# Moving the start addresses of the split weights and of the activations inside SBUF

## The chip, the cores and the metric

The kernel runs on one core of one Trainium2 chip. The metric is the device time of one execution in microseconds (us); lower is better. A change below 0.2% of it can't be told from no change.

## The reference, cut to what matters

Two layers of a network and a third block with its MLP are computed in float32 for 256 tokens of width 2048. Nearly all the arithmetic is in products of an activation (256 tokens by up to 8192 features) with a weight matrix that is read once from memory:

```
proj = h @ w_in                                      # layer 0: 2048 x 10272
return x + jnp.concatenate([y_a, y_b, y_m], axis=-1) @ w_out
...
proj = h @ w_in                                      # layer 1: 2048 x 4416
q = (rms_norm(c_q, mla_q_norm_w) @ mla_w_uq)
kv = (rms_norm(c_kv, mla_kv_norm_w) @ mla_w_ukv)
return x + jnp.concatenate([y_c, y_m], axis=-1) @ w_out
...
# block 2: retention with w_in (2048 x 12288) and w_out (4096 x 2048),
# then an MLP with w_up (2048 x 8192), relu squared, w_down (8192 x 2048)
```

Between the products stand norms, short convolutions, a state-space scan in chunks, and three kinds of attention.

## The kernel before

**One stream of weights.** `PLAN` lists every block of weight columns in the order in which it is worked. A block is a *job*; a job is cut into *sub-jobs* of at most 1024 float32 columns per partition. For each sub-job the kernel issues a DMA into a buffer `raw`, splits the weights into two parts, and multiplies. `run_stream` writes this order out by hand: splits run two sub-jobs ahead of the matmuls, DMAs up to three more.

**The split.** A product of float32 numbers is made from three products of a faster format (`F32R`): a number x is hi + lo, where hi is x cast to the format by ScalarE (ACT) and lo = x - hi comes from VectorE (DVE). `emit_split` puts both parts of a sub-job into one buffer `w` of 2112 elements per partition, hi from element `WOFF` = 20 and lo from `WOFF` + 1024. There are `N_SPLIT` = 4 such buffers. The activations are kept the same way: a `Feat` holds, for two blocks of 128 features, hi (256 tokens) and lo (256 tokens) side by side in a buffer of pool `unit`.

**Two layouts.** `emit_mm` issues the matmuls of a sub-job. The first operand of `mm` is the *stationary* one (128 x 128, loaded into the array before the matmul), the second the *moving* one (128 partitions by its columns):

```
if kind == "A":
    trio = ((dst, wh, xb), (dst[:, 0:256], wl, xh))
elif kind == "A3":
    trio = ((dst, wh, xh), (dst, wh, xl), (dst, wl, xh))
else:
    sh, sl = xh[:, t * 128:t * 128 + 128], xl[:, t * 128:t * 128 + 128]
    trio = ((dst, sh, wh), (dst, sh, wl), (dst, sl, wh))
```

- **A**: the weights are stationary. A pair of matmuls: weights hi against the activation's hi and lo together (512 columns), then weights lo against the activation's hi (256 columns).
- **A3**: the same in three matmuls of 256 columns (jobs `uq`, and half of `ukv`).
- **B**: the activations are stationary, the weights move: three matmuls of 512 columns (352, 384 or 288 in a few jobs, 256 in half of `ukv`).

In the trace, names stand as output<-moving,stationary: `g<-h,w` has the weights stationary, `g<-w,h`, `g<-w,y`, `g<-w,yr` and `g<-w,hid` have them moving (`g<-w,mem` and `g<-mem,w` are the same for the memory input).

**Where things lie.** Pools are laid one after the other in each partition. Their sizes give the start of each buffer; *phase* is that start modulo 256 bytes. The buffers of `w` are 8448 bytes (33 x 256), so all four start at one phase, 128. Buffers of `unit` (4096 bytes) and `half` (2048 bytes) hold the activations, and also all operands of the attentions; they start at one phase too, and slices inside them lie 512 or 1024 bytes apart. The pool of constants stands between `w` and `unit`, so its total size sets their phase. Before the change: both weight parts at 128 + 4 x 20 = 208, all buffers of `unit` and `half` at 192, the identity and other square constants (`sq`, `trs_r`) at 128, the key table `ks` at 160.

Of the kernel before, what the change touches and what calls it, by code (L numbers as in the profile page):

```python
# [19 lines left out]
N_HALF = 15  # L20
N_SPLIT = 4
AHEAD = 2
WOFF = 20
MLP_PARTS = (6, 5, 5)


# [89 lines left out]
def block_kernel(ctx, tc, a, out):  # L116
# [14 lines left out]
    def nm(s):  # L131
        serial[0] += 1
        return f"{s}_{serial[0]}"
# [10 lines left out]
    def C(shape, name, dt=F32):  # L144
        return cst.tile(shape, dt, name=name)

    def bank(shape, name):

        while free_banks[0] == 0:
            yield  # L150
        free_banks[0] -= 1
        return psb.tile(shape, F32, tag="b", name=nm(name))

    def rel():
        free_banks[0] += 1
# [20 lines left out]
    def mm(o, l, r, start, stop=True):  # L176
        nc.tensor.matmul(o, l, r, start=start, stop=stop, skip_group_check=True)  # L177
# [5 lines left out]
    def split_to(hi, lo, x):  # L183
        nc.scalar.copy(hi, x)  # L184
        tt(lo, x, hi.bitcast(F32), ALU.subtract)
# [2 lines left out]
    sq = C([128, 3, 128], "sq")  # L188
    ident, tri, cmask = (sq[:, i, :] for i in range(3))
    trs_r = C([128, 128], "trs_r", F32R)  # L190
    ones = C([128, 8], "ones")
    mhalf = C([128, 8], "mhalf")
    pv = C([128, NVEC], "pv")
    invf = C([128, 2], "invf")
    hv = C([128, 3, 32], "hv")
# [7 lines left out]
    o = 0  # L203
# [125 lines left out]
    def emit_split(m):  # L329
        s = subs[m]  # L330
        n, nc_ = s.n, s.job.ncols
        src = raws[(s.job.key, s.gi)][:, s.s0:s.s0 + n, :]

        hl = wsp.tile([128, 2112], F32R, tag="w", name=nm("w"))
        pitch = {352: 512, 288: 320}.get(nc_, nc_)
        hv_, lv_ = (hl[:, WOFF + i * 1024:WOFF + i * 1024 + n * pitch].rearrange(
            "p (k c) -> p k c", c=pitch)[:, :, 0:nc_] for i in range(2))
        split_to(hv_, lv_, src)
        splits[m] = (hv_, lv_)

# [34 lines left out]
    def run_stream():  # L375
# [15 lines left out]
        for m, s in enumerate(subs):  # L391
            if s.first and s.job.key in hooks:
                hooks[s.job.key]()
            while at["split"] < n and at["split"] <= m + (min(AHEAD, m) if m < n - 4 else 3):
                dma_to(at["split"])
                emit_split(at["split"])
                at["split"] += 1
            dma_to(min(at["split"] + 3, m + 3))
            drive(lambda: all(k in s.job.x.done for k in range(s.k0 + s.s0, s.k0 + s.s0 + s.n)))
            if m < n - 2:  # L400
                emit_mm(m)
                del splits[m]
                if s.last:
                    spawn(s.job.post(s.job.ps))
                step_tasks()
# [45 lines left out]
    def rstd_from(dst, sums, n, ncols):  # L451
        v = S([128, ncols])
        ts(v, sums, 1.0 / n, EPS, ALU.mult, ALU.add)
        nc.gpsimd.tensor_tensor(dst, v, mhalf[:, 0:ncols], ALU.pow)  # L454
# [25 lines left out]
    def feat_rstd(dst, sqs, n):  # L480

        acc = sqs[0]
        nc.gpsimd.tensor_tensor(acc[:, 0:2, :], acc[:, 0:2, :], acc[:, 2:4, :], ALU.add)
        nc.gpsimd.tensor_tensor(acc[:, 0, :], acc[:, 0, :], acc[:, 1, :], ALU.add)
        yield
        yield
        ps = yield from bank([128, 2, 128], "fs")
        for t in range(2):
            mm(ps[:, t, 0:8], acc[:, 0, t * 128:(t + 1) * 128], ones, start=(t == 0))
        yield  # L490
        rstd_from(dst, ps[:, :, 0], n, 2)
        rel()
        yield
# [119 lines left out]
    def prep_mem():  # L613
        sqs = []
        for u in range(4):
            memt.alloc(u)
            for kp, nk in ((0, 1), (1, 1), (2, 2)) if u == 0 else ((0, 2), (2, 2)):
                memt.write_scaled(u * 4 + kp, nk, lambda k: memu[u][:, kp + k, :],
                                  lambda k: col("mem_norm_w", u * 4 + kp + k))
                memt.mark(u, kp, nk)  # L620
                yield
            s = U([128, 4, 256], F32, "msq")
            act(s, memu.pop(u), AF.Square)
            add_up(sqs, s)
        yield from feat_rstd(stat[:, RM, :], sqs, D)
        rbm = H([128, 256], F32, "rbm")
        yield from bcast_rows(rbm, stat[:, RM, :])
        L0["rbm"] = rbm

    def prep_x():  # L630
        yield from wait(7)
        xu, sqs = [], []
        for u in range(4):
            xu.append(load_t(a["xt"], u, "xt"))
            yield from wait(2)
            s = U([128, 4, 256], F32, "xsq")
            act(s, xu[u], AF.Square)
            add_up(sqs, s)
        r0 = S([128, 2])
        yield from feat_rstd(r0, sqs, D)  # L640
        rb0 = H([128, 256], F32, "rb0")
        yield from bcast_rows(rb0, r0)
        yield
        for u in range(4):
            h0.alloc(u)
            for kp in (0, 2):
                nc.gpsimd.tensor_tensor(xu[u][:, kp:kp + 2, :], xu[u][:, kp:kp + 2, :],
                                        rb0.unsqueeze(1).to_broadcast([128, 2, 256]), ALU.mult)
                yield
                h0.write_scaled(u * 4 + kp, 2, lambda k: xu[u][:, kp + k, :],  # L650
                                lambda k: col("norm0_w", u * 4 + kp + k))
                h0.mark(u, kp, 2)
# [185 lines left out]
    def ssd_group(g):  # L838
# [73 lines left out]
        yield  # L912
        rg = S([128, 2])
        yield from feat_rstd(rg, [s2], 512)
        rb = H([128, 256], F32, "rbg")
        yield from bcast_rows(rb, rg)
# [488 lines left out]
    for entry in PLAN:  # L1405
        key = entry[0]
        kind, rest = key[0], key[1:]
        n = len(entry[3])
# [114 lines left out]
```

## Time and profile before

| | |
|---|---|
| time of three runs | 2674.33, 2674.76, 2675.19 us (median 2674.76) |
| the profiled execution | 2674.39 us, of which 2672.6 us is the span of its instructions |
| granted TensorE clock | 0.999 of the full 2.4 GHz |
| TensorE matmul (PE) busy | 2651.7 us, 14136 matmuls |
| TensorE weight load (PEld) busy | 2280.1 us |
| DVE, ACT, POOL busy | 1638.7, 1299.1, 141.6 us |
| DMA | 488.86 MB, mean 183 GB/s |

A matmul's busy time in the trace overlaps that of the next one, since they are pipelined. How long one really takes of TensorE's time is read from the distance between the starts of neighbours: in a merged row of the timeline, the length less the duration of the last matmul, divided by the count less one.

### The profile page before, as it was taken

What the parts mean: (1) busy time and instruction counts of PE and PEld (TensorE: products, weight loads), DVE (VectorE), ACT (ScalarE), POOL (GpSimd) and SP (SyncE); (2) the same over time, 40 slices, a digit from 0 to 9 for tenths busy, and PEclk for the clock granted to TensorE, in tenths of its full rate; (3) what the DMA queues carried; (4) which work ended last, traced back from release to release, by engine and by line L of the source; (5) the groups of instructions that cost most, each with busy time, mean ns of one, the idle gap of its engine ahead of it and who ended that gap; (6) DMA issues with size and microseconds to landing.
All of it is one profiled execution on the core that took longest, in us unless ns stands there. A gap on an engine that the chain in (4) does not pass through costs nothing.

```text
span 2672.6 us, 34737 instructions
## 1 busy us (share of the span) xinstructions
PE 2651.7 (99%) x14136; PEld 2280.1 (85%) x14136; DVE 1638.7 (61%) x2066; ACT 1299.1 (49%) x1772; POOL 141.6 (5%) x104
## 2 busy tenths in 40 slices
PE   8999999999999999999999999999999999999998
PEld 7998888888899999888888888888888888888886
DVE  6757787655546887646565555555555545545554
ACT  5556555544444666544444343444455434534543
POOL 4100232000000000000000000000000000000000
PEclk9999999999999999999999999999999999999999
DMA  7454444565545444455444455454455555555553
GB/s 268 173 188 170 158 158 159 188 221 193 187 152 204 148 150 174 173 190 206 176 174 183 178 189 186 179 193 172 178 186 190 190 189 189 189 190 188 189 207 139
DMA packets 74688, 488.86 MB, mean 183 GB/s; under 512 B 8864, under 2 KB 10656, under 8 KB 20384
## 3 DMA queue, kind: packets, MB, share of 16 engines
q1 hardware_dynamic: 74528, 486.64, 50.2%
q8 instruction: 110, 1.80, 0.3%
q14 instruction: 50, 0.41, 0.0%
HBM read 484.51 MB, written 2.10 MB: 182 GB/s over the span
## 4 chain that ended last, share of the span: by engine, by line
PE 97%; ACT 1%; DVE 1%; DMA 0%; issue 0%; SPq 0%; POOLq 0%; POOL 0%; DVEq 0%; ACTq 0%
PE g L177 92%; PE tr L425 1%; PE ro L177 1%; PE at.s L177 1%; ACT w L184 0%; DMA raw<-in_mem_v_dram 0%; PE rs L177 0%; PE at.o L177 0%; DVE w L162 0%; PE yd L177 0%; PE seg L177 0%; DVE xbc L171 0%; PE ma.s L177 0%; PE ma.o L177 0%; PE at.t L1168 0%
## 5 line engine op out<-in xcount | busy, mean ns | idle before, releaser
L162 DVE TENSOR_TENSOR w<-raw,w 128x1024 fp32r<-128x1024 f32 (+4 forms) x929 | 1115.3, 1211 | 850.1 <-ACT w L184 849.4
L184 ACT CAST w<-raw 128x1024 fp32r<-128x1024 f32 (+4 forms) x929 | 936.6, 1026 | 681.2 <-PE g L177 663.4
L177 PE MATMUL g<-h,w 128*128 128x512 f32 (+1 forms) x6144 | 1084.3, 337 | 1.0 <-DVE qx L162 1.0
L177 PEld LDWEIGHTS g<-h,w 128*128 128x128 f32 x6144 | 941.8, 188 | 125.8 <-issue 2.0
L177 PE MATMUL g<-w,h 128*128 128x512 f32 (+3 forms) x2208 | 468.0, 372 | 0.0
L177 PEld LDWEIGHTS g<-w,h 128*128 128x128 f32 x2208 | 392.5, 188 | 65.9
L177 PE MATMUL g<-w,hid 128*128 128x512 f32 x1536 | 356.6, 394 | 0.8 <-DVE x L171 0.8
L177 PEld LDWEIGHTS g<-w,hid 128*128 128x128 f32 x1536 | 288.5, 188 | 68.1 <-DVE x L171 1.3
L177 PE MATMUL g<-w,y 128*128 128x512 f32 x1152 | 269.9, 395 | 0.0
L177 PEld LDWEIGHTS g<-w,y 128*128 128x128 f32 x1152 | 215.6, 188 | 49.6 <-ACT y L184 0.4
L284 ACT COPY low<-g 128x512 f32<-128x512 f32 x100 | 58.8, 588 | 343.5 <-PE g L177 343.5
L177 PE MATMUL g<-w,yr 128*128 128x512 f32 x768 | 179.8, 395 | 0.0
L177 PEld LDWEIGHTS g<-w,yr 128*128 128x128 f32 x768 | 144.0, 188 | 33.0
L162 DVE TENSOR_TENSOR x<-x,g 128x512 f32<-128x512 f32 x48 | 30.8, 684 | 71.3 <-PE g L177 71.3
L162 DVE TENSOR_TENSOR blk<-g,low 128x512 f32<-128x512 f32 x100 | 68.3, 683 | 0.4 <-PE g L177 0.4
L177 PE MATMUL g<-w,mem 128*128 128x512 f32 x192 | 50.2, 420 | 8.6 <-ACT mem L174 7.2
L1303 POOL TENSOR_TENSOR s<-s,mhalf 128x1 f32<-128x1 f32 x16 | 22.6, 1412 | 608.9 <-DVE s L166 608.9
L177 PEld LDWEIGHTS g<-w,mem 128*128 128x128 f32 x192 | 37.9, 201 | 19.6 <-ACT mem L174 8.1
L177 PE MATMUL g<-cq,w 128*128 128x256 f32 x432 | 54.5, 282 | 0.0
L454 POOL TENSOR_TENSOR stat<-s,mhalf 128x2 f32<-128x2 f32 x7 | 10.1, 1446 | 828.9 <-DVE s L168 828.9
L177 PEld LDWEIGHTS g<-cq,w 128*128 128x128 f32 x432 | 52.3, 188 | 0.1
L174 ACT ACT_TABLE_LOAD x28 | 35.9, 1283 | 20.5 <-PE pre L177 10.5
(264 smaller groups left out, 1450.3 us busy)
## 6 DMA issues: line engine op xcount, KB each, us to landing
raw<-in_w_in_dram SPq DMA_DIRECT2D x96, 1024.0 KB, 4.8
raw<-in_ret_w_in_dram SPq DMA_DIRECT2D x96, 1024.0 KB, 4.8
raw<-in_mlp_w_up_dram SPq DMA_DIRECT2D x64, 1024.0 KB, 4.8
raw<-in_mlp_w_down_dram SPq DMA_DIRECT2D x64, 1024.0 KB, 4.8
raw<-in_w_out_dram SPq DMA_DIRECT2D x48, 1024.0 KB, 4.8
raw<-in_ret_w_out_dram SPq DMA_DIRECT2D x32, 1024.0 KB, 4.8
raw<-in_w_in_dram SPq DMA_DIRECT2D x12, 704.0 KB, 4.0
raw<-in_mem_k_dram SPq DMA_DIRECT2D x8, 1024.0 KB, 4.8
```

The lines of the kernel that those rows point to most:

```text
L162: nc.vector.tensor_tensor(o, x, y, op)
L174: nc.scalar.activation(o, x, f, **kw)
L177: nc.tensor.matmul(o, l, r, start=start, stop=stop, skip_group_check=True)
L184: nc.scalar.copy(hi, x)
L284: nc.scalar.copy(low, ps[:, :, 256:512])
L425: nc.tensor.transpose(ps[:, i, t * 128:(t + 1) * 128], src(t, kp + i), ident)
L454: nc.gpsimd.tensor_tensor(dst, v, mhalf[:, 0:ncols], ALU.pow)
L1303: nc.gpsimd.tensor_tensor(r, vv, mhalf[:, 0:1], ALU.pow)
```

## The change

`WOFF` goes. The weight parts now start at offsets that depend on the layout: jobs of kinds in `A_KINDS` (weights stationary) put hi at element 1048 and lo at element 12, the others (weights moving) hi at 1032 and lo at 8. Two constants of 8 columns, `ones` and `mhalf`, become halves of one tile `om` of 8 columns, which makes the pool of constants 32 bytes smaller; the sums over partitions in `feat_rstd` use 4 columns instead of 8.

```diff
-WOFF = 20
+PHASES = {"A": (1024 + 24, 12), "B": (1024 + 8, 8)}
+A_KINDS = ("mk", "B", "C", "xs", "sz", "sc", "mq", "mz", "uq", "ukv", "zc", "q", "k", "up")
...
-    ones = C([128, 8], "ones")
-    mhalf = C([128, 8], "mhalf")
+    om = C([128, 8], "om")
+    ones, mhalf = om[:, 0:4], om[:, 4:8]
...
-        hv_, lv_ = (hl[:, WOFF + i * 1024:WOFF + i * 1024 + n * pitch].rearrange(
-            "p (k c) -> p k c", c=pitch)[:, :, 0:nc_] for i in range(2))
+        hv_, lv_ = (hl[:, o:o + n * pitch].rearrange("p (k c) -> p k c", c=pitch)[:, :, 0:nc_]
+                    for o in PHASES["A" if s.job.key[0] in A_KINDS else "B"])
...
-            mm(ps[:, t, 0:8], acc[:, 0, t * 128:(t + 1) * 128], ones, start=(t == 0))
+            mm(ps[:, t, 0:4], acc[:, 0, t * 128:(t + 1) * 128], ones, start=(t == 0))
```

On every engine the instructions stand in the same order before and after; only the width of those twelve small sums and of two memsets changes, and the addresses:

| operand, start modulo 256 bytes | before | after |
|---|---|---|
| weights, stationary: hi / lo | 208 / 208 | 224 / 176 |
| weights, moving: hi / lo | 208 / 208 | 160 / 160 |
| activations and all buffers of `unit` and `half` | 192 | 160 |
| `ks` | 160 | 128 |
| `sq`, `trs_r` | 128 | 128 |

## Rows read from the trace of the kernel before

**Rows 1.** The page: span; busy time of each engine, share, instructions.

```profile
span 2672.6 us, 34737 instructions
PE 2651.7 (99%) x14136; PEld 2280.1 (85%) x14136; DVE 1638.7 (61%) x2066; ACT 1299.1 (49%) x1772; POOL 141.6 (5%) x104
```

**Rows 2.** The page: the chain that ended last, by engine.

```profile
PE 97%; ACT 1%; DVE 1%; DMA 0%; issue 0%; SPq 0%; POOLq 0%; POOL 0%; DVEq 0%; ACTq 0%
```

**Rows 3.** Waits of PE: who for whom, total us, times, longest.

```profile
PE g L177 <- ACT mem L174: 7.2, 3, 5.9
PE ma.t L534 <- DVE p L166: 1.3, 1, 1.3
```

**Rows 4.** Groups of PE by shape: busy us, mean ns, then idle before.

```profile
L177 PE MATMUL g<-h,w 128*128 128x512 f32 x3072 | 1073.6, 393 | 1.0 <-DVE qx L162 1.0
L177 PE MATMUL g<-h,w 128*128 128x256 f32 x3072 | 863.0, 281 | 0.0
L177 PE MATMUL g<-w,h 128*128 128x512 f32 x1536 | 361.3, 395 | 0.0
L177 PE MATMUL g<-w,hid 128*128 128x512 f32 x1536 | 356.6, 394 | 0.8 <-DVE x L171 0.8
L177 PE MATMUL g<-w,y 128*128 128x512 f32 x1152 | 269.9, 395 | 0.0
L177 PE MATMUL g<-w,yr 128*128 128x512 f32 x768 | 179.8, 395 | 0.0
L177 PE MATMUL g<-cq,w 128*128 128x256 f32 x432 | 54.5, 282 | 0.0
L177 PE MATMUL g<-w,mem 128*128 128x512 f32 x192 | 50.2, 420 | 8.6 <-ACT mem L174 7.2 <-DVE mem L171 0.9 <-DVE w L162 0.4
L177 PE MATMUL g<-mem,w 128*128 128x512 f32 x128 | 44.7, 393 | 0.0
L177 PE MATMUL g<-ck,w 128*128 128x256 f32 x192 | 28.5, 284 | 0.0
```

**Rows 5.** Timeline of PE, layout A in the MLP: start, length, group, count.

```profile
1959.80 100.47 PE L177 MATMUL g<-h,w 128*128 128x256 f32 x579
```

**Rows 6.** Timeline of PE, layout B in the MLP.

```profile
2089.80 90.51 PE L177 MATMUL g<-w,hid 128*128 128x512 f32 x390
```

**Rows 7.** Busy time by stretch in A and B: PE, PEld, DVE, ACT, POOL; PEclk.

```profile
1954.00:2084.00 130.00, 130.00 (x753) 115.28 (x752) 74.97 (x80) 65.53 (x80) 1.60 (x1) 1.00 0.53 188
2090.00:2180.00 90.00, 90.00 (x390) 73.03 (x389) 45.05 (x40) 35.52 (x36) 0.00 (x0) 1.00 0.55 198
```

**Rows 8.** Timeline of PE: a job of layout A3 (`uq`).

```profile
886.56 4.42 PE L177 MATMUL g<-cq,w 128*128 128x256 f32 x36
```

**Rows 9.** Timeline of PE: six matmuls `ro`, both operands at phase 192.

```profile
1621.77 0.39 PE L177 MATMUL ro<-vh,sh 128*128 128x512 f32 x1
1622.00 0.40 PE L177 MATMUL ro<-vl,sh 128*128 128x512 f32 x1
1622.23 0.40 PE L177 MATMUL ro<-vh,sl 128*128 128x512 f32 x1
1622.47 0.39 PE L177 MATMUL ro<-vh,sh 128*128 128x512 f32 x1
1622.69 0.39 PE L177 MATMUL ro<-vl,sh 128*128 128x512 f32 x1
1622.93 0.40 PE L177 MATMUL ro<-vh,sl 128*128 128x512 f32 x1
```

**Rows 10.** Timeline of PE: moving constants at 128 against stationary data at 192.

```profile
717.63 1.03 PE L425 MATMUL tr<-sq,x 128*128 128x128 f32 x8
272.75 1.06 PE L177 MATMUL pre<-sq,dax 128*128 128x128 f32 x8
```

**Rows 11.** Timeline of PE: `ks` moving at 160 against 192, and the next.

```profile
1026.58 0.28 PE L177 MATMUL at.s<-ks,qs 128*128 128x256 f32 x1
1026.70 0.51 PE L177 MATMUL at.s<-kk,q 128*128 128x256 f32 x3
```

**Rows 12.** Timeline of PE: `rs`, plain float32, 256 columns, all at 192.

```profile
1277.70 1.02 PE L177 MATMUL rs<-q,k 128*128 128x256 f32 x4
```

**Rows 13.** Groups by shape: the split of a full sub-job on DVE and ACT.

```profile
L162 DVE TENSOR_TENSOR w<-raw,w 128x1024 fp32r<-128x1024 f32 x847 | 1043.9, 1242 | 777.4 <-ACT w L184 777.0
L184 ACT CAST w<-raw 128x1024 fp32r<-128x1024 f32 x847 | 874.0, 1049 | 642.0 <-PE g L177 628.3 <-DMA raw<-in_mem_v_dram 5.4 <-ACT w L184 5.0
```

## The prediction

> **What bounds the kernel now.** I read the page first: of the span, PE holds 99% [rows 1], and 97% of the chain that ended last is PE's [rows 2]. Then I asked what PE waits for: the longest entry is 7.2 us at the start, the next 1.3 us [rows 3]. So nothing that happens on DVE, ACT or the DMA queues sets the end; the time is the sum over 14136 matmuls of the distance from one start to the next. The change can only act by making that distance shorter or longer.
>
> These distances come from merged rows of the timeline. In layout A, 579 matmuls take 100.47 us [rows 5]; less the last one's 0.28 (its mean duration, [rows 4]) and over 578 steps that is 173.3 ns each, or 346.7 ns for a pair of 512 and 256 columns. In layout B, 390 matmuls take 90.51 us [rows 6]: (90.51 - 0.39) / 389 = 231.7 ns for 512 columns. A job of A3, all of 256 columns, has 36 in 4.42 us [rows 8]: (4.42 - 0.28) / 35 = 118.3 ns. With 118.3 for the 256 columns, the 512 of an A pair take 346.7 - 118.3 = 228.4 ns. The granted clock in both stretches is 1.00 [rows 7], the level of 2.4 GHz. At one column per cycle (an estimate) 512 columns would be 213.3 ns and 256 would be 106.7 ns. So there are some 15 ns over the stream in A's first matmul, 11.6 in its second, 18.4 in B. This excess is what an address could move.
>
> How much of it there is: A pairs are 3072 + 128 = 3200 and B matmuls of 512 columns 1536 + 1536 + 1152 + 768 + 192 = 5184 [rows 4]. Excess in A: 3200 x (346.7 - 320.0) = 85 us; in B: 5184 x 18.4 = 95 us. These 180 us, 6.7% of the time, are the ceiling of any gain in the two main layouts.
>
> **Does the excess depend on addresses?** While a matmul streams its moving operand, the stationary operand of the next one is loaded: PEld is busy 115.28 of 130 us in A [rows 7]. Two streams then read SBUF at once. One row says the excess is not a fixed price of a matmul: `rs` is plain float32, 256 columns, and takes (1.02 - 0.38) / 3 = 213 ns, which is just 512 cycles at 2.4 GHz (an estimate again), with no excess to be seen at the rounding of the row [rows 12]. Its columns enter at half the rate, and at half the rate the excess is gone. That speaks for two streams that get in each other's way at the full rate.
>
> The Trainium skill, page "TensorE: Matmul & The Clock Gate", section "Part 2: What happens when you issue a matmul", says otherwise: PE has two independent read ports, and loading the next weights takes nothing from the running matmul; its section "Back-to-back issue gap" gives N/2.4 + 2.5 ns, which would be 215.8 ns for 512 columns. The trace has 231.7 [rows 6], so the gap rule does not hold here; whether the port rule does is the question of the change. By that rule the sum would be zero.
>
> **The change part by part.** The unit of my argument is the difference d = phase of the moving operand less phase of the stationary operand that is loaded meanwhile, since this says where two streams that start together stand to each other.
>
> 1. *A, first matmul* (512 columns; the weights' lo is loaded). d was 192 - 208 = -16; it is 160 - 176 = -16. By d nothing changes: 0.
>
> 2. *A, second matmul* (256 columns; the next weights' hi is loaded). d was -16, it becomes 160 - 224 = -64. Two rows have d = -64: the transposes `tr` (identity at 128 moving, data at 192 stationary) with (1.03 - 0.27) / 7 = 108.6 ns, and `pre` with (1.06 - 0.28) / 7 = 111.4 ns [rows 10]. They have 128 columns, so it is the load that paces them and not the stream; but a 256-column matmul needs 106.7 ns for its stream and the same load of 128 columns beside it, so if neither is held up it takes what these rows take. From both sides, then: 108.6 (a gain of 9.7 ns) and 111.4 (a gain of 6.9), and at worst none. I take the middle of the two rows, 110.0, a gain of 8.3 ns. There are 3200 such matmuls in the A pairs, and in A3 two of three load hi next: 2/3 x (432 + 192) = 416 [rows 4]. 3616 x 8.3 = 30.0 us less.
>
> 3. *B* (5184 matmuls of 512). d was 208 - 192 = 16; it becomes 160 - 160 = 0. The row with d = 0 and 512 columns is `ro`: five steps from 1621.77 to 1622.93, 1.16 / 5 = 232.0 ns [rows 9], against 231.7 now. 5184 x 0.3 = 1.6 us more, which is nothing within the rounding. Bounds: the shortest step in those rows, 220 (from 1622.47 to 1622.69), and the longest, 240, though neither holds for many in a row.
>
> 4. *The narrower B jobs and the attentions.* The widths 352, 384 and 288 follow B: zero. In the attentions both operands lie in `unit` or `half` and move together; `ks` goes from 160 to 128 while its partner goes from 192 to 160. No d changes there: zero.
>
> 5. *The sums with 4 columns instead of 8, and the common tile `om`.* Twelve sums; the memsets stand at the very start, where PE waits for the memory input anyway [rows 3]. Zero.
>
> 6. *The split.* ACT and DVE write the same sizes to other addresses. DVE takes 1242 ns and ACT 1049 for a full sub-job [rows 13]; such a sub-job feeds PE for 8 pairs, 8 x 346.7 = 2774 ns. They could take half as long again before PE would wait; in the A stretch DVE is busy 74.97 of 130 us [rows 7]. Covered, zero; without this cover each nanosecond per split would cost 847 ns in all.
>
> Sum: 2674.39 (the profiled execution) - 30.0 + 1.6 = 2646.0. That execution lies 0.4 us under the median, so I forecast **2646 us**. With the two rows of step 2 as ends, its own range is 2674.4 - 35.1 + 1.6 = 2641 to 2674.4 - 25.0 + 1.6 = 2651; the rounding of the rows of `ro` (10 ns over five steps, 2 ns a matmul, 10 us in all) widens it to 2631 to 2661.
>
> **The rivals.**
>
> *B gains too.* If equal phases let the two streams run in step, so that they never ask for the same place at once, B's 231.7 falls as well. For it: `rs`, also at d = 0, shows no excess [rows 12]. Against it: `ro`, at the full rate, shows all of it [rows 9]. Price: down to the 213.3 of the bare stream it would be 95 us; halfway, 9.2 x 5184 = 48 us, the time 2646 - 1.6 - 48 = 2597. At the pace of A's first matmul (228.4) it would be 17 us, the time 2627.
>
> *Nothing happens.* The excess belongs to the full-rate stream alone, wherever it starts, and d plays no part. For it: 231.7 at d = 16, 232.0 at d = 0 and 228.4 at d = -16 are within 4 ns [rows 5, 6, 9]; `pre` and `tr` differ by 3 ns at one d [rows 10]. Time: 2675. The port rule of the Trainium skill, page "TensorE: Matmul & The Clock Gate", quoted above, says this too.
>
> *Slower: the moving stream dislikes the phase 160 itself.* Before the change one moving operand of TensorE lies at 160, `ks`: its step from 1026.58 to 1026.70 is 120 ns for 256 columns [rows 11], against 118.3 at 192 [rows 8]. If that is the phase and not the rounding, all moving streams now pay it: 1.7 ns per 256 columns, 5.1 per A pair (16 us) and 3.4 per B matmul (18 us), so 34 us more, 2709. It decides against the change as soon as a full-width B matmul takes 5.8 ns more than now with step 2 as I have it (30.0 us over 5184). Against it: the row's rounding alone is as large as the effect.
>
> **How the numbers follow.** My case: 0.40. B gains too: 0.22. Nothing: 0.18. Slower: 0.20, since the absolute phase of every moving stream changes and only one coarse row speaks to it. Faster by over 0.2% (5 us; less can't be told from no change in this kernel) is then 0.62, within 0.2% 0.18, slower 0.20. The range reaches to 2600, which leaves out the far part of the second case, and up to 2688, which takes in "nothing" and the nearer part of the slower case (half of its 34 us is 2692); about 0.1 is left out at either end.
>
> **What would show it.** In the profile after, PE should still wait for nothing. The A stretch of the MLP should have more matmuls per 100 us: 346.7 - 8.3 = 338.4 ns a pair, so about 591 in place of 579. The B stretch should keep its 390 in 90 us; 400 or more would show the second case, fewer than 386 the last. `uq` should fall from 118.3 to about 113 on the mean of its three. `ro`, `tr` and `pre`, whose d stays, should keep their steps; if they move, it is the absolute phase that counts and my unit d is wrong. The prediction is wrong if what a stream pays depends on where it starts rather than on its distance to the other, or if the rows with 128 columns say nothing about 256.

## The result and the profile after

| | before | after |
|---|---|---|
| median of four runs each | 2674.55 us (2673.77 to 2675.19) | 2643.15 us (2642.60 to 2643.27) |
| ratio, 95% interval | | 0.9882 [0.9865, 0.9899] |
| profiled execution, its span | 2674.39, 2672.6 us | 2643.22, 2641.4 us |
| its granted TensorE clock | 0.999 | 0.998 |

The kernel is 31.4 us faster, 1.2%. The forecast was 2646. The profile shows that the total came out near it for reasons other than those forecast.

The page of the kernel after: span, busy time of each engine, and the chain that ended last by engine. They answer to [rows 1, 2].

```profile
span 2641.4 us, 34737 instructions
...
PE 2620.3 (99%) x14136; PEld 2271.6 (86%) x14136; DVE 1639.1 (62%) x2066; ACT 1299.0 (49%) x1772; POOL 141.5 (5%) x104
...
PE 97%; ACT 1%; DVE 1%; DMA 0%; issue 0%; SPq 0%; POOLq 0%; POOL 0%; DVEq 0%; ACTq 0%
```

Waits of PE after (who for whom, total us, times, longest), for [rows 3]:

```profile
PE g L180 <- ACT mem L177: 7.3, 3, 5.8
PE ma.t L537 <- DVE p L169: 1.4, 1, 1.4
```

PE still has 99% of the span and 97% of the chain, and waits for nothing new; DVE, ACT and POOL are as busy as they were. So the 31 us come out of the distance from one matmul to the next. The timeline of PE after (start, length, group, count) shows where. The first row is uq [rows 8], the second layout B [rows 6], the third layout A in the place of [rows 5]; the other two are layout A elsewhere, where the pairs of the kernel before took 346.7 ns as well.

```profile
880.89 4.40 PE L180 MATMUL g<-cq,w 128*128 128x256 f32 x36
...
2072.71 107.60 PE L180 MATMUL g<-w,hid 128*128 128x512 f32 x474
...
1959.80 100.46 PE L180 MATMUL g<-h,w 128*128 128x512 f32 x590
...
494.82 85.44 PE L180 MATMUL g<-h,w 128*128 128x256 f32 x492
...
2414.83 105.55 PE L180 MATMUL g<-h,w 128*128 128x256 f32 x608
```

The reader takes the last matmul's duration off each length and divides by the count less one, as the prediction did. A merged row names the shape of its first matmul; in A the two shapes alternate, so with an odd count the last is of the same shape (0.39 or 0.28 us), with an even count of the other, and a pair comes out to some 0.2 ns. B: (107.60 - 0.39) / 473 = 226.7 ns, where it was 231.7. A in the first part of the MLP: twice (100.46 - 0.28) / 589, a pair of 340.2 ns, where it was 346.7. But A at 494 us and at 2414 us gives twice (85.44 - 0.39) / 491 and twice (105.55 - 0.39) / 607, pairs of 346.4 and 346.5, no faster than before to that accuracy. And `uq` takes (4.40 - 0.28) / 35 = 117.7 ns against 118.3.

Counted over all neighbours in the two traces by their starts (steps of B under 260 ns and pairs of A under 400, so that stalls are left out), the mean B step went from 231.65 to 226.91 ns and the mean A pair, from one 512-column start to the next, from 346.87 to 344.69. That is 4.74 x 5184 = 24.6 us from B and 2.18 x 3200 = 7.0 us from A, together 31.6 against the 31.4 measured. In A, 984 of 3059 pairs take at most 342 ns, where 4 did before, and 1902 still take 343 to 347. The small B widths hardly moved: 384 columns from 175.6 to 173.6 ns, 352 stayed at 160.0, 288 went from 130.5 to 131.7.

The busy time per group says the same more roughly. Groups of PE by shape after (busy us, mean ns, then idle before), for [rows 4]:

```profile
L180 PE MATMUL g<-h,w 128*128 128x512 f32 x3072 | 1066.7, 392 | 1.0 <-DVE qx L165 1.0
L180 PE MATMUL g<-h,w 128*128 128x256 f32 x3072 | 857.0, 279 | 0.0
...
L180 PE MATMUL g<-w,hid 128*128 128x512 f32 x1536 | 349.0, 389 | 0.8 <-DVE x L174 0.8
```

The B group falls by 356.6 - 349.0 = 7.6 us for 1536 matmuls, 4.9 each; the two A groups by 6.9 and 6.0 us for 3072 pairs, 4.2 a pair at the most. Busy times of pipelined matmuls overlap, so only the starts give the true size.

Last, the six `ro` of [rows 9], whose operands both lie at one phase before and after. Timeline of PE after:

```profile
1331.11 0.39 PE L180 MATMUL ro<-vh,sh 128*128 128x512 f32 x1
1331.34 0.39 PE L180 MATMUL ro<-vl,sh 128*128 128x512 f32 x1
1331.56 0.39 PE L180 MATMUL ro<-vh,sl 128*128 128x512 f32 x1
1331.79 0.39 PE L180 MATMUL ro<-vh,sh 128*128 128x512 f32 x1
1332.02 0.39 PE L180 MATMUL ro<-vl,sh 128*128 128x512 f32 x1
1332.24 0.39 PE L180 MATMUL ro<-vh,sl 128*128 128x512 f32 x1
```

Five steps in 1.13 us are 226 ns each, where they were 232. Nothing about these six changed but the absolute phase (192 to 160). By the prediction's own sign, absolute phase would then count. Or they follow the matmuls around them. The experiments had to settle that.

### The profile page after: what moved, and what is told of

Its sections match the earlier page's. It is cut to its first block, busy times and chain, and to the rows that moved or that the text cites. A ratio compares the mean times of both kernels' runs of the same rounds, so it can differ in the third digit from the quotient of the medians.

```text
span 2641.4 us, 34737 instructions
## 1 busy us (share of the span) xinstructions
PE 2620.3 (99%) x14136; PEld 2271.6 (86%) x14136; DVE 1639.1 (62%) x2066; ACT 1299.0 (49%) x1772; POOL 141.5 (5%) x104
## 4 chain that ended last, share of the span: by engine, by line
PE 97%; ACT 1%; DVE 1%; DMA 0%; issue 0%; SPq 0%; POOLq 0%; POOL 0%; DVEq 0%; ACTq 0%
PE g L180 92%; PE tr L428 1%; PE ro L180 1%; PE at.s L180 1%; DMA raw<-in_mem_v_dram 0%; ACT w L187 0%; PE rs L180 0%; PE at.o L180 0%; DVE w L165 0%; PE yd L180 0%; PE seg L180 0%; DVE xbc L174 0%; PE ma.o L180 0%; PE ma.s L180 0%; PE at.t L1171 0%
## 5 line engine op out<-in xcount | busy, mean ns | idle before, releaser
L180 PE MATMUL g<-w,h 128*128 128x512 f32 (+3 forms) x2208 | 460.8, 368 | 0.0
L180 PE MATMUL g<-w,hid 128*128 128x512 f32 x1536 | 349.0, 389 | 0.8 <-DVE x L174 0.8
L180 PE MATMUL g<-w,y 128*128 128x512 f32 x1152 | 264.5, 390 | 0.0
L1306 POOL TENSOR_TENSOR s<-s,om 128x1 f32<-128x1 f32 x16 | 22.6, 1412 | 598.6 <-DVE s L169 598.6
L457 POOL TENSOR_TENSOR stat<-s,om 128x2 f32<-128x2 f32 x7 | 10.1, 1446 | 819.7 <-DVE s L171 819.7
```

The lines of the kernel that those rows point to most:

```text
L1306: nc.gpsimd.tensor_tensor(r, vv, mhalf[:, 0:1], ALU.pow)
```

## The experiments

The theory after the result: **what counts is the difference d (phase of the moving operand less phase of the stationary one loaded beside it), and in B d = 0 is the good place.** The rivals: the absolute phase 160 of the moving stream is good; or the gain comes from A's two weight phases and B's is a by-product. All kernels below are the changed kernel with one edit. Times are medians; ratios are to the kernel before, with 95% intervals.

### Each half of the change by itself

The activations at 160 with the weights left at 208, then the weights moved with the activations left at 192:

```diff
-PHASES = {"A": (1024 + 24, 12), "B": (1024 + 8, 8)}
+PHASES = {"A": (20, 1024 + 20), "B": (20, 1024 + 20)}
```

```diff
-    om = C([128, 8], "om")
-    ones, mhalf = om[:, 0:4], om[:, 4:8]
+    ones = C([128, 8], "ones")
+    mhalf = C([128, 8], "mhalf")
...
-            mm(ps[:, t, 0:4], acc[:, 0, t * 128:(t + 1) * 128], ones, start=(t == 0))
+            mm(ps[:, t, 0:8], acc[:, 0, t * 128:(t + 1) * 128], ones, start=(t == 0))
```

> Weights back at 208/208 in both layouts as before the change, activations at 160 as after it. In layout B the moving stream then starts at 208 and the stationary load at 160 (difference 48); in A the moving stream at 160, the load at 208 (difference -48). If the start of the stationary load decides in B, B takes 226.7 ns as after the change and the time is about 2674.5 - 5184 x 5 ns = 2649 us. If the start of the moving stream decides, B stays at 231.7 and the time is 2674 give or take what A does. If only the pair of 160 against 160 helps, also 2674. If the difference alone decides (the prediction's unit), B is at a value not seen yet.

> Weights at 224/176 and 160/160 as after the change, activations left at 192 as before it. In layout B the moving stream starts at 160, the load at 192 (difference -32). If the start of the moving stream decides, B takes 226.7 ns and the time is about 2649 us. If that of the stationary load decides, B stays at 231.7 and the time is about 2674. If the pair is needed, also 2674. In A the moving stream is at 192, the load at 176 and 224.

Measured: act_only 2683.19 us, 1.0033 [1.0021, 1.0045]; w_only 2682.60 us, 1.0031 [1.0019, 1.0043]. Each half alone makes the kernel slower, by 8.9 and 8.3 us. Timeline of PE in layout B, of act_only:

```profile
2344.70 95.60 PE L180 MATMUL g<-w,hid 128*128 128x512 f32 x409
```

and of w_only:

```profile
2344.75 95.60 PE L180 MATMUL g<-w,hid 128*128 128x512 f32 x409
```

Both give (95.60 - 0.39) / 408 = 233.4 ns: d is +48 in the first (208 - 160) and -32 in the second (160 - 192). Over the trace the mean B step rose by 1.60 ns in act_only; 1.60 x 5184 = 8.3 us, nearly the whole loss, and A's mean pair stands where it was (346.92 in act_only, 346.82 in w_only). In w_only B's weights do lie at 160, and B is slow: absolute phase 160 of the moving stream is not what helps.

### Each layout by itself

The weights back at 208 in A (b_only), then in B (a_only):

```diff
-PHASES = {"A": (1024 + 24, 12), "B": (1024 + 8, 8)}
+PHASES = {"A": (20, 1024 + 20), "B": (1024 + 8, 8)}
```

```diff
-PHASES = {"A": (1024 + 24, 12), "B": (1024 + 8, 8)}
+PHASES = {"A": (1024 + 24, 12), "B": (20, 1024 + 20)}
```

> As after the change, but the stationary weights of layout A back at 208/208. If the gain is B's (5184 matmuls from 231.7 to 226.7 ns, 26 us), the time is about 2649 us and A keeps 346.7 ns a pair, with no stretch at 340. If the prediction's step on A carried it, the time stays near 2674.

> As after the change, but the moving weights of layout B back at 208/208. A's weights are at 224/176. If A's second matmul carried the gain as the prediction had it, the time is about 2646 us. If A only has stretches at 340 ns a pair among those at 346.7 (about a third of the pairs after the change, some 7 us), the time is about 2668, less if a stationary load at 160 helps B by itself, which would give 2642.

Measured: b_only 2650.10 us, 0.991 [0.9895, 0.9924]; a_only 2675.32 us, 1.0004 [0.9995, 1.0014]. Timeline of PE, of b_only (a row of A, a row of B):

```profile
1959.69 100.58 PE L180 MATMUL g<-h,w 128*128 128x512 f32 x579
...
2317.61 92.64 PE L180 MATMUL g<-w,hid 128*128 128x512 f32 x408
```

and of a_only (B):

```profile
2339.68 90.69 PE L180 MATMUL g<-w,hid 128*128 128x512 f32 x388
```

With d = 0 in B alone the step is (92.64 - 0.39) / 407 = 226.7 ns and A's pair is twice (100.58 - 0.39) / 578 = 346.7: b_only is 24.2 us faster than the kernel before, so most of the 31.4 us is B's. In a_only A's phases alone give 6.1 us (pair 344.95 on the mean), and B takes 6.5 back: the expectation of about 2668 left out that the old weights beside the moved activations put B at d = +48, as in act_only. The two layouts add up, since the matmuls stand one behind the other.

### A map of phases

To see what d does over its whole range, every B job gets a phase of its own for both parts, in three kernels with the activations at 160, 192 and 224. In A, one of the two parts is spread in the same way (in the last two both parts of `up` together):

```diff
+def offsets(hi, lo):
+    h, l = ((p - 128) % 256 // 4 for p in (hi, lo))
+    return (h, 1024 + l) if h <= l else (1024 + h, l)
+def shuffled(i):
+    return 16 * ((5 * i + 2) % 16)
...
-                    for o in PHASES["A" if s.job.key[0] in A_KINDS else "B"])
+                    for o in offsets(*phases(s.job.key)))
```

`phases` gives a job of B `shuffled(i)` for hi and lo, i being the job's number in its row of jobs. The activations are moved by the width of `om`: 8, 16 or 24 columns.

> A map and no candidate. Activations at 160. Each job of layout B (v, g, rout, out0, out1, down) has both weight parts at a phase of its own, all 16 multiples of 16 bytes in turn; the A jobs up have hi at each of the 16 with lo at 176, the A jobs q, k, sc have lo at each of the 16 with hi at 224. If the pair of exact starts counts in B, only 160 gives 226.7 ns and 208 gives 232.9 as in the runs before; if there is a band of good phases, neighbours (144, 176) are near 227 too. If something with a period below 256 bytes is behind it (64 or 128), 96 or 32 and 224 are as good as 160. In A, if 340 ns a pair belongs to hi at 224, the other phases of hi have only 346.7; if it is a rhythm that any phase can fall into, several show it.

> The same map with the activations at 192; the A jobs up have hi and lo at one phase. If only the difference between the two streams counts, B's steps are those of the map at 160 moved by 32 bytes, so the best is at 192 with 226.7 ns. If the absolute starts count, 192 gives about 231.5 (as ro had at 192 against 192 before the change), 160 gives 233.3 and 208 gives 231.7, and the best may be elsewhere.

> The same map with the activations at 224, which is 160 plus 64. If what counts repeats every 64 bytes, B's steps are those of the map at 160 with the phase moved by 64 (best at 224, 226.7 ns), and also those at 160 with no shift if each stream's start counts modulo 64 by itself. If it repeats only at 256 bytes, 224 against 224 is no better than the rest.

Measured (one run each, so that only steps inside the traces are compared): 2679.15, 2685.08 and 2685.43 us. Timeline of PE in map_160, B jobs at d = +16, 0, +80 and -16:

```profile
2369.71 15.46 PE L206 MATMUL g<-w,hid 128*128 128x512 f32 x66
...
2564.82 15.35 PE L206 MATMUL g<-w,hid 128*128 128x512 f32 x67
...
2589.65 16.57 PE L206 MATMUL g<-w,hid 128*128 128x512 f32 x71
...
2647.78 12.47 PE L206 MATMUL g<-w,hid 128*128 128x512 f32 x52
```

and in map_192, at d = +32 (the weights at 224), 0 and -16:

```profile
1911.63 6.70 PE L206 MATMUL g<-w,yr 128*128 128x512 f32 x28
...
2169.83 20.34 PE L206 MATMUL g<-w,hid 128*128 128x512 f32 x89
...
2374.71 16.49 PE L206 MATMUL g<-w,hid 128*128 128x512 f32 x69
```

The first fence gives 231.8, 226.7, 231.1 and 236.9 ns, the second 233.7, 226.7 and 236.8. Counted over the starts of all jobs at one d, from the thirteenth step of each job on:

| d | activations 160 | 192 | 224 |
|---|---|---|---|
| 0 | 226.9 | 226.8 | 227.1 |
| +16 | 231.6 | 231.4 | 231.6 |
| -16 | 236.2 | 236.5 | 234.9 |
| +32 | 233.3 | 233.3 | 233.3 |

At nine other values the jobs of all three maps agree within 1.5 ns, and lie between 231.0 and 234.7. The last three values have two paces: at +112 some jobs ran at 226.7 and others at 231.1, at +64 some at 228.9 and others at 233.3, at +48 one at 230.0 and the others at 233.3. Timeline of PE in map_192, two jobs at d = +64:

```profile
1767.70 20.70 PE L206 MATMUL g<-w,h 128*128 128x512 f32 x88
...
2395.72 24.65 PE L206 MATMUL g<-w,hid 128*128 128x512 f32 x107
```

They run at 233.4 and 228.9 ns. So in B it is d that counts, whatever the absolute phase, but at a few values of d it leaves two paces open. Before the change (d = +16) B stood at one of the better places already, and d = 0 is the only one at which every job settled near 226.7.

In A the first map has 720 pairs of at most 342 ns, the other two 41 and 28. Several phases show that pace, not hi at 224 with lo at 176 alone: in the first map the two jobs with lo at 144 and the two with lo at 48 run at 340.0, and so does `up` with hi at 96.

The maps also show what happens where a job begins. In map_160 a job at d = 0 behind one at phase 32 begins with steps of 231, 227, 226, 227, 227, 226 ns; in map_192 one behind a job at phase 112 begins with 254, 240, 235, 233, 236, 224, 231, 236, 228, 233, 230, 227: it can need a dozen matmuls to settle. `ro` is three or six matmuls among long B jobs, and the traces show that it goes with these and not with its absolute phase: 231.5 ns on the mean beside B at 231.7 before the change and 226.7 beside 226.9 after it, but 230.4 in a_only, with its operands at 160 as after the change and B at 233.

### Everything moved by 32 bytes

The last word on absolute phase: all differences as in the changed kernel, all absolute phases 32 bytes further.

```diff
-PHASES = {"A": (1024 + 24, 12), "B": (1024 + 8, 8)}
+PHASES = {"A": (1024 + 32, 20), "B": (1024 + 16, 16)}
...
-    om = C([128, 8], "om")
+    om = C([128, 16], "om")
```

> All operands of the changed kernel moved by 32 bytes: activations back at 192 as before the change, moving weights at 192, stationary weights at 0 (hi) and 208 (lo). If only the difference between the two streams counts, B keeps 226.7 ns and the time is that of the changed kernel, 2643 us, within the few us that A's rhythm decides. If the absolute starts count (160 against 160), B is back near 231.7 and the time near 2669.

Measured: 2642.62 us, 0.9883 [0.9868, 0.9897], within 0.02% of the changed kernel. Timeline of PE (A, B, A):

```profile
1959.84 80.40 PE L180 MATMUL g<-h,w 128*128 128x256 f32 x472
...
2309.74 90.60 PE L180 MATMUL g<-w,hid 128*128 128x512 f32 x399
...
2414.77 95.50 PE L180 MATMUL g<-h,w 128*128 128x512 f32 x550
```

A's pairs are 339.7 and 346.9 ns in the same two places in which the changed kernel has 340.2 and 346.5, and B is at 226.7. `ro`, back at phase 192, takes 226.8 ns on the mean. The unit d holds in A and in B.

### What the two phases of A do

In the changed kernel A's d is -16 in the first matmul and -64 in the second. One of the two is changed at a time: lo to 144 (d = +16), lo to 48 (d = +112), hi to 96 (d = +64).

```diff
-PHASES = {"A": (1024 + 24, 12), "B": (1024 + 8, 8)}
+PHASES = {"A": (1024 + 24, 4), "B": (1024 + 8, 8)}
```

```diff
-PHASES = {"A": (1024 + 24, 12), "B": (1024 + 8, 8)}
+PHASES = {"A": (24, 1024 + 44), "B": (1024 + 8, 8)}
```

```diff
-PHASES = {"A": (1024 + 24, 12), "B": (1024 + 8, 8)}
+PHASES = {"A": (1024 + 56, 12), "B": (1024 + 8, 8)}
```

> The changed kernel with the stationary lo at 144 in place of 176. If the map's two jobs at 340.0 ns a pair stand for all (a phase pair that always falls into the fast rhythm), nearly all A pairs take 340 ns: the 70% that take 346.7 in the changed kernel gain 6.7 ns, 2200 x 6.7 = 15 us, so 2628 us. If the rhythm is kept or lost by chance of the entry, as with lo at 176, about 2643.

> The changed kernel with the stationary lo at 48 in place of 176: like the kernel before, 2628 us if this pair always falls into the rhythm of 340 ns, about 2643 if not. 48 lies 128 bytes from 176, so a time like that of the changed kernel would also be what a repeat after 128 bytes gives.

> The changed kernel with the stationary hi at 96 in place of 224 (lo stays at 176): 2628 us if this pair always falls into the rhythm of 340 ns, about 2643 if not; 96 lies 128 bytes from 224.

Measured: a_lo144 2642.56 us, 0.9882 [0.9868, 0.9897]; a_lo48 2642.31, 0.9882 [0.9867, 0.9896]; a_hi96 2652.21, 0.9918 [0.9902, 0.9935]. B stays at 226.9 in all three. Two totals are the changed kernel's within 0.9 us, and yet the traces are not alike. Timeline of PE in a_lo144, two places of layout A:

```profile
493.73 86.49 PE L180 MATMUL g<-h,w 128*128 128x256 f32 x489
...
2414.76 95.48 PE L180 MATMUL g<-h,w 128*128 128x256 f32 x561
```

the same of a_lo48:

```profile
493.74 86.52 PE L180 MATMUL g<-h,w 128*128 128x256 f32 x508
...
2414.71 90.46 PE L180 MATMUL g<-h,w 128*128 128x512 f32 x516
```

and of a_hi96:

```profile
1959.77 90.60 PE L180 MATMUL g<-h,w 128*128 128x256 f32 x532
...
2424.78 95.44 PE L180 MATMUL g<-h,w 128*128 128x512 f32 x539
```

In pairs: 353.3 and 340.0 in a_lo144, 339.8 and 350.2 in a_lo48, 339.8 and 353.3 in a_hi96. Within one kernel the same shapes at the same phases run for 90 us at one pace in one place and at another pace elsewhere. So a pair of phases doesn't fix A's pace; it fixes which paces there are (340.0 and 346.7 ns in the changed kernel, 340.0 and 353.3 in a_lo144 and a_hi96, 340.0 and 350.0 in a_lo48 are the common ones), and the place in the program decides which of them is taken. What runs ahead is part of it: a_only has the changed kernel's phases in all of A and differs only in B's weights, and yet its A in the first part of the MLP runs at another pace (each of the two was profiled once). Timeline of PE in a_only, to set beside the third row of the profile after:

```profile
1959.83 100.35 PE L180 MATMUL g<-h,w 128*128 128x512 f32 x578
```

That is twice (100.35 - 0.28) / 577 = 346.9 ns a pair, where the changed kernel has 340.2; the `q` and `k` of the pairs 2 and 3, at 346.7 in the changed kernel, run at 340.0 in a_only. That the places repeat from run to run is likely from the times (the four runs of each kernel lie within 1.7 us of each other), and the version below rests on it. With hi at 96 the slow pace took more of the stretches (mean pair 347.67); the means are 344.50 in a_lo144 and 344.26 in a_lo48, against 344.69 in the changed kernel.

### A version that takes the good pace in each place

If the places are reproducible, each job can have the phases that ran fast there: lo at 48 for most of A, lo at 144 for `mk`, `up` and the `q` and `k` of three of four pairs.

```diff
-PHASES = {"A": (1024 + 24, 12), "B": (1024 + 8, 8)}
+PHASES = {"A": (24, 1024 + 44), "A2": (1024 + 24, 4), "B": (1024 + 8, 8)}
+def layout(key):
+    if key[0] not in A_KINDS:
+        return "B"
+    return "A2" if key[0] in ("mk", "up") or (key[0] in ("q", "k") and key[1] != 1) else "A"
...
-                    for o in PHASES["A" if s.job.key[0] in A_KINDS else "B"])
+                    for o in PHASES[layout(s.job.key)])
```

> Two phase pairs for the stationary weights, each where its run had the rhythm of 340 ns a pair: hi 224 with lo 144 in the jobs mk, up and the q, k of the pairs 0, 2 and 3; hi 224 with lo 48 in the other A jobs. B as in the changed kernel. If the rhythm that a block of A jobs falls into is set by its phase pair and by the job ahead of it, and is then kept (hysteresis), most A pairs take 340: the mean pair falls from 344.9 ns to about 341.5, 3200 x 3.4 = 11 us, so 2632 us. If the rhythm is a matter of chance from run to run, the mean stays near 344.5 and the time near 2642.

Measured: 2633.81 us (2633.10 to 2633.99, five runs), 0.9846 [0.9833, 0.986]. Timeline of PE, the two places of a_lo144 and a_lo48:

```profile
493.79 76.44 PE L186 MATMUL g<-h,w 128*128 128x256 f32 x449
...
2409.82 90.38 PE L186 MATMUL g<-h,w 128*128 128x256 f32 x531
```

Both are at 340.0 ns a pair now, and 2610 of the 3059 pairs counted take at most 342 ns. The mean pair is 341.47: 5.40 x 3200 = 17.3 us from A and 24.6 from B, together 41.9 against 40.8 measured. This version beats both kernels, by 40.8 us the one before and by 9.3 us the changed one.

## Why the prediction came out as it did

- **What bounds the kernel**: right. PE's own steps are the time; the means of the steps, times their counts, account for every kernel's time within about 1.3 us.
- **The unit d**: right, by `shifted` and the maps, though in A, and in B at a few values, d leaves more than one pace open. The signs that were to test it were not right. `ro` went from 232 to 226 ns with its d unchanged, and by the prediction's words that spoke for the absolute phase; but `ro` goes with the B jobs around it, as `shifted` and `a_only` show. And the d of `tr` and `pre` did not stay, as the prediction has it: their identity lies at 128 before and after and their data moved from 192 to 160, so it went from -64 to -32. Their mean steps stayed within 0.1 ns of 108.9 and 111.7 all the same.
- **Step 3, B**: the step that failed first. It was put at +1.6 us and gave -24.6. The price of d = 0 was read from five steps of `ro` [rows 9], and these had the pace of the B jobs around them. The rival *B gains too* had the condition, equal phases, and, at 2627 to 2597, a size for it (why equal phases help is not shown); B's 226.9 ns is 4.7 under the old pace where that rival's nearer form had 3.3.
- **Step 2, A's second matmul**: the mechanism was forecast as one price for d = -64, 30.0 us less. It gave 7.0 in the pairs and (118.3 - 117.7) x 432 = 0.3 us in `uq`, which was to fall to 113. `tr` and `pre` [rows 10] were the wrong scale: their steps of 128 columns did not answer to the change of d, while a pair whose second matmul is at d = -64 runs mostly at 340.0 or at 346.7 ns, and only 32% of the pairs took the faster. The A stretch that the prediction named as its sign showed 590 matmuls for the forecast 591, but that was one of the places that happen to run fast; the two other rows of A shown above did not move.
- **Step 1, A's first matmul at an unchanged d**: can't be priced apart from step 2. Where A runs at 340, the starts give 226.7 ns for 512 columns and 113.3 for 256; where it runs at 346.7, 229.2 and 117.5. Both matmuls of a pair move together.
- **Steps 4, 5 and 6**: right within 0.4 us. The 384-column jobs gave 2.0 x 192 = 0.4 us, the 288-column ones took 0.2 back; PE waits for no split.
- **The sum**: -28.4 forecast, -31.4 measured. Two wrong terms, 23 us too much in A and 26 too little in B, cancelled, and that the total fits is luck. Taken one by one they would have failed: in `a_only` A gained 6.1 us where step 2 promised 30, and `b_only` gained 24 where step 3 promised nothing.
- **Nothing happens**: false; the same instructions in the same order take from 226.7 to 236.9 ns by the phase alone. The port rule of the Trainium skill, page "TensorE: Matmul & The Clock Gate", section "Part 2: What happens when you issue a matmul", doesn't agree with these rows at the full rate.
- **The moving stream dislikes phase 160**: false. `shifted` has it at 192 and takes the same time.

What stays open: which part of SBUF or of TensorE the two streams meet in, and how the work ahead of a job decides which pace is taken. Both would need a kernel of nothing but matmuls with one thing varied at its entry; that wasn't tried.

## What to carry to other kernels

When TensorE is back to back and yet over its column count, look at where the moving and the stationary operand start modulo 256 bytes: here equal phases for a 512-column moving operand were worth 2% of each matmul, and moving only one of the two operands cost time. Read the price of a layout from a stretch of many matmuls with nothing else between them, never from a handful in a row, whose steps may still be those of the work ahead of them. And forecast the parts of a change one by one and test them one by one: a total that fits can hide two errors of its own size.

## What the runs showed of the hardware that was not expected

- The steps come in levels. Outside the maps, settled A pairs mostly take 340.0, 346.7, 350.0 or 353.3 ns, and in the maps B takes 233.3 at many values of d and 226.7 at d = 0. The levels are 3.33 or 6.67 ns apart, 8 or 16 cycles at 2.4 GHz (an estimate from the granted clock of 1.00).
- A stretch keeps the pace on which it has settled. It held over rows of 75 to 105 us, and the same phases ran at 353.3 and at 340.0 in one execution of a_lo144.
- The phases of one layout change the pace of the other: with A's phases untouched, moving B's weights from 160 to 208 turned one A stretch from 340.2 to 346.9 ns a pair (a_only).
- Opposite signs of d are not alike: in B +16 gives 231.6 ns and -16 gives 236.2, in all three maps the minus is the worse.
